# Two sums for the first layer's experts, and the next layer's preparation ahead of the last down projection

## The chip, the cores and the metric

The kernel runs on one core of one Trainium2 chip. The metric is the device time of one execution in microseconds; the time before is the median of three runs.

## What is computed

The reference is a backbone of two layers over 512 latent tokens and 256 context tokens of 1024 numbers. Layer 0 mixes tokens by pooling, layer 1 by grouped-query attention (16 query heads, 4 key/value heads of 64). Behind each mixer stands a mixture of 16 SwiGLU experts of width 256, two of which take each token. Every sub-layer has its own shift, scale and gate, six vectors per layer from a 1024 x 6144 matrix.

```python
for i in range(DEPTH):
    sh1, sc1, g1, sh2, sc2, g2 = adaln(c, w_mod[i], b_mod[i])
    a_lat = modulate(x, norm1_g[i], sh1, sc1)
...
    x = x + g1 * y_lat
    x = x + g2 * hier_moe(modulate(x, norm2_g[i], sh2, sc2), ...)
```

```python
a = jnp.einsum('nd,edf->nef', hf, w_gate)
b = jnp.einsum('nd,edf->nef', hf, w_up)
hid = jax.nn.silu(a) * b * gates.astype(h.dtype)[..., None]
return jnp.einsum('nef,efd->nd', hid, w_down).reshape(shp)
```

Layer 0 runs over all 768 rows (context first, two tiles of 128 rows, then four latent tiles). In layer 1 the context only gives keys and values.

## The kernel before

All is float32. A large product splits each operand into a rounded high part (ScalarE's cast, L464) and a low rest (VectorE's subtraction, L465) and takes three matmuls (`mm3`, L468 to L470).

**Weights.** Each weight load is 1 MB and goes through SP's queue in one fixed order (`order`). `fill` issues the next one as soon as a slot is free; `cap` says how many slots may be used. Behind the first layer's experts the order is: key weights (`qkv` 4), value weights (`qkv` 5), the modulation chunks 2 and 3 of layer 1 (two halves each), the four query weights.

**Modulation.** `mod_row` makes one chunk of 512 modulation numbers: 16 matmuls L404 on two halves of weights, a bias matmul L409, a cast on ScalarE (L411), a subtraction on VectorE (L413). `mod_spread` brings a chunk to all partitions: a matmul L426 for latent and context each, then a copy (L429) for the shift, or for the scale a product with the norm's gain (L395, L423, L431).

**Experts.** `place` finds each expert's rows, `fetch` gathers them from hD by an indirect DMA on POOL's queue (L726), `turn` transposes and splits them, `ups_steps` splits the weights, `up` does gate and up projection (L468 to L470), `turn_hidden` transposes the hidden rows. `down` takes the gate product on VectorE (L767) into one of two y buffers, eight matmuls L772, two products L773, and adds y to accD in DRAM by an indirect DMA that accumulates (L774, the scatter). In turn e the loop runs up(e), turn(e+1), down(e-1), turn_hidden(e); the last down, of expert 15, stands behind the loop. accD holds the residual rows, written by the pooling stage (L961); every scatter of the layer goes to it, so each waits until the one before has landed.

**Hooks.** `experts` calls functions at given turns. Before, chunks 0 and 1 of layer 1's modulation come at turns 13 and 14; `last`, behind the last down, splits key and value weights (`split_w`) and makes chunks 2 and 3. Then follows a loop for overflowing experts, whose number of turns is read at run time; at its end all engines meet. It runs no turn with these inputs.

**Start of layer 1.** Behind that loop `load_rows` brings row tiles of accD, `mod_spread` spreads the four chunks, and for each tile `norm` (a square sum on ScalarE, L446, and a root, L1159), `prep` (VectorE), `turn_rows` (transposes, casts, subtractions) and the projections to keys and values follow. The key projection of tile 0 is the first `mm3` of the layer.

Of the kernel before, what the change touches and what calls it, by code (L numbers as in the profile page):

```python
# [20 lines left out]
D = 1024  # L21
S = 512
L = 256
NT = 6
# [17 lines left out]
BESIDE = (4, 6)  # L42
CAPS = dict(pool=6, moe0=(7,) * 11 + (5,), qkv=4, query=2, attend=(2, 2, 3, 4), wo=3, moe1=(7, 7, 6, 5))

# [181 lines left out]
def backbone(ctx: ExitStack, tc: tile.TileContext, a: dict, out: bass.AP):  # L226
# [244 lines left out]

    hD = dram.tile([NT * 128, D], F32, name="hD")
    accD = dram.tile([NT * 128, D], F32, name="accD")


    class Moe:
# [187 lines left out]
        def up_units(self, e):  # L664
            while len(self.ring) < 6:
                self.more_units()
            return [self.ring[(4 * e + q) % 6] for q in range(4)]

# [92 lines left out]
        def down(self, e, hT, wd):  # L761
# [6 lines left out]
            for half in range(2):  # L768
                cols = slice(512 * half, 512 * half + 512)
                p = pb.get("y", [n, 512])  # L770
                for k in range(2):
                    T.matmul(p, hT[:, k, :], wd[:, k, cols], start=k == 0, stop=k == 1)  # L772
                V.tensor_mul(y[:, cols], p, gs[:, cols])  # L773
            G.indirect_dma_start(out=self.acc, out_offset=bass.IndirectOffsetOnAxis(ap=self.slots[e][0], axis=0),  # L774
                                 in_=y, in_offset=None, bounds_check=self.nt * 128 - 1, oob_is_err=False,
# [162 lines left out]
    def pooled(t):  # L938
# [20 lines left out]
        if t == NT - 1:  # L959
            done("pool")  # L960
        nc.sync.dma_start(accD[t * 128:t * 128 + 128, :], x[t])  # L961

    def norm2(t):
# [98 lines left out]

    sm = ar.scope()
    mod1 = partB + [sm.tile([128, 512], F32R) for _ in range(2)]
    wkv = {}

    def mod1_row(*chunks):
        for c in chunks:
            for _ in mod_row(1, c, mod1[c]):
                pass  # L1070

    def last():
        state["until"] = ("qkv", 0)
        cap(CAPS["qkv"])
        for c in (4, 5):
            wkv[c] = [split_w(c, q) for q in range(4)]
        ar.swap("mid")
        for _ in range(2):
            m0.more_units()
        mod1_row(2, 3)  # L1080

    m0.experts(accD, CAPS["moe0"], more, {
        11: tables, 12: lambda: state.update(mid=0), 13: lambda: mod1_row(0), 14: lambda: mod1_row(1), NE: last})
    m0.sb.free()
# [5 lines left out]
    vv = ab.tile([128, NT, 256])  # L1090
    sx = ar.scope()
    xb = [sx.tile([128, D]) for t in range(4)]
    x = [xb[t % 4] for t in range(NT)]

    def load_rows(t):
        nc.sync.dma_start(x[t], accD[t * 128:t * 128 + 128, :])

    for t in range(4):
        load_rows(t)
    fill()  # L1100
    bc = {(n, v): sx.tile([128, D]) for n in ("B", "A") for v in range(2)}
    pb.split(m=(4, 1), t=(4, 1))
    for c in range(4):
        for _ in mod_spread(sm, 1, c // 2, c % 2, mod1[c], {v: bc["BA"[c // 2], v] for v in range(2)}):
            pass
    sm.free()
# [79 lines left out]
    def store_key(t):  # L1186
        for kv in range(0, 4, 2):
# [3 lines left out]
            A.copy(kT[:, kv:kv + 2, :, t * 128:t * 128 + 128], p2.rearrange("p (a b) c -> p a b c", a=2))  # L1191

    norm(0)
    norm(1)
    prep(0)
    norm(2)
    prep(1)
    turn_rows(0)
    load_rows(4)
    for t in range(NT):  # L1200
        PK[t] = pb.get("k", [128, 256])
        project(PK[t], t, wK)
        if t:
            key(t - 1)
            A.copy(vv[:, t - 1, :], PV[t - 1])
        if t + 1 < NT:
            turn_rows(t + 1)
            if t + 5 < NT:
                load_rows(t + 5)
        square_heads(sk, PK[t], ks[:, t, :])  # L1210
        A.activation(ks[:, t, :], ks[:, t, :], AF.Sqrt, scale=1.0 / HEAD, bias=eps)
        norm(t + 3)
        prep(t + 2)
        PV[t] = pb.get("v", [128, 256])
        project(PV[t], t, wV)
        if t:
            store_key(t - 1)
# [232 lines left out]
    m1.route()  # L1450
    m1.experts(o_rows, CAPS["moe1"], more)
    m1.sb.free()
# [40 lines left out]
```

## Time and profile before

| what | value |
|---|---|
| runs | 931.27 us median (929.12 to 934.59) |
| profiled execution | 933.5 us, span 931.7 us |
| TensorE (PE) | 799.8 us, 86% of the span |
| VectorE (DVE) | 614.5 us, 66% |
| ScalarE (ACT) | 479.1 us, 51% |
| GpSimd (POOL) | 175.4 us, 19% |
| DMA | 204.80 MB, mean 220 GB/s |

The share of busy time is an average over stages with different limits, so a change is read from the stage in which it lies: the experts of layer 0 run from about 150 to 331 us, the preparation of layer 1 from there to about 380. In a timeline a row gives start, duration, engine, line and operation, and in brackets how long the engine was idle before and what ended that. A time is counted from the start of the span. L12 is line 12 of the kernel before.

### The profile page before, as it was taken

To read this page: it belongs to the slowest core of one execution; us is meant where nothing else is said; L and a number is where in the kernel's file an instruction comes from. 1 tells how busy PE (TensorE), PEld (TensorE's weight loads), DVE (VectorE), ACT (ScalarE), POOL (GpSimd) and SP (SyncE) were. 2 spreads that over 40 slices of the span, in tenths; PEclk is the share of its full clock that TensorE was granted. 3 is DMA by queue.
4 is the path that set the end of the run, shared out by engine and by line. 5 is a ranking of instruction groups with operands and counts; after the bars stand their busy time and mean duration, and the time that the engine had idled before them with its cause. 6 is when DMAs were issued, how large, how long until landed. Compare 5 with 4: busy or idle time off the path is not lost. (4 is left out here: it accounts for less than half of the span.)

```text
span 931.7 us, 12772 instructions
## 1 busy us (share of the span) xinstructions
PE 799.8 (86%) x4593; PEld 543.3 (58%) x4593; DVE 614.5 (66%) x1077; ACT 479.1 (51%) x1003; POOL 175.4 (19%) x164
## 2 busy tenths in 40 slices
PE   4699947989998864998787999999999489999993
PEld 0256725566776431997776666556677255566561
DVE  3552875799988734665666677768536768888761
ACT  2534344445555323565558777768623454455440
POOL 1051332122233410002310000001200312322211
PEclk9899976999999995899999999999999789999997
DMA  8997388799999887301100434220136789899962
GB/s 330 417 361 299 136 299 325 262 321 358 370 359 304 311 239 264 126 1 57 80 2 0 181 100 172 91 91 1 46 148 269 282 291 325 305 338 338 345 218 31
DMA packets 36722, 204.80 MB, mean 220 GB/s; under 512 B 6660, under 2 KB 6740, under 8 KB 16816
## 3 DMA queue, kind: packets, MB, share of 16 engines
q1 hardware_dynamic: 24976, 172.06, 48.4%
q0 software_dynamic: 10032, 27.30, 11.6%
q10 hardware_dynamic: 1648, 4.60, 1.3%
q8 instruction: 37, 0.61, 0.3%
q14 instruction: 29, 0.24, 0.1%
HBM read 187.15 MB, written 25.17 MB: 228 GB/s over the span
## 5 line engine op out<-in xcount | busy, mean ns | idle before, releaser
L468 PE MATMUL banks<-low 128*128 128x512 f32 (+2 forms) x404 | 155.1, 384 | 5.7 <-DVE main L1142 4.4
L469 PE MATMUL banks<-low 128*128 128x512 f32 (+2 forms) x404 | 150.2, 372 | 1.1 <-DVE low L465 1.1
L470 PE MATMUL banks<-low 128*128 128x512 f32 (+2 forms) x404 | 150.1, 372 | 0.0
L465 DVE TENSOR_TENSOR low<-main,low 128x1024 fp32r<-128x1024 f32 (+1 forms) x119 | 127.7, 1131 | 14.9 <-ACT low L464 14.7
L464 ACT CAST low<-main 128x1024 fp32r<-128x1024 f32 (+1 forms) x135 | 117.0, 930 | 2.3 <-issue 1.3
L1329 DVE TENSOR_REDUCE main<-banks 128x1 f32<-128x768 f32 x64 | 61.2, 956 | 43.5 <-PE banks L1325 43.3
L468 PEld LDWEIGHTS banks<-low 128*128 128x128 f32 (+1 forms) x404 | 74.6, 185 | 24.1 <-ACT low L464 6.5
L772 PE MATMUL banks<-main 128*128 128x512 f32 (+1 forms) x176 | 82.6, 614 | 3.3 <-ACT low L464 3.3
L469 PEld LDWEIGHTS banks<-low 128*128 128x128 f32 (+1 forms) x404 | 74.7, 185 | 16.2 <-DVE low L465 1.7
L470 PEld LDWEIGHTS banks<-low 128*128 128x128 f32 (+1 forms) x404 | 74.2, 184 | 16.9 <-DVE low L465 0.4
L1347 ACT COPY main<-banks 128x384 f32<-128x384 f32 x128 | 55.9, 486 | 33.6 <-PE banks L1346 33.2
L465 POOL TENSOR_TENSOR low<-main,low 128x512 fp32r<-128x512 f32 x16 | 20.7, 1296 | 273.5 <-ACT low L464 273.5
L404 PE MATMUL banks<-main,cT 128*32 128x512 f32 x376 | 56.8, 707 | 15.0 <-DVE low L413 7.1
L1350 ACT ACTIVATE main<-banks,main 128x768 f32<-128x768 f32 x64 | 63.7, 995 | 8.1 <-DVE main L1333 3.3
L758 ACT COPY main<-banks 128x256 f32<-128x256 f32 (+1 forms) x32 | 11.1, 346 | 100.7 <-PE banks L756 93.2
L773 DVE TENSOR_TENSOR main<-banks,main 128x512 f32<-128x512 f32 (+1 forms) x64 | 42.7, 686 | 27.6 <-PE banks L772 26.0
L459 PE MATMUL banks<-ident,main 128*128 128x128 f32 (+2 forms) x384 | 50.0, 274 | 12.7 <-DVE main L1167 5.5
L1346 PE MATMUL banks<-ident,main 128*128 128x128 f32 x384 | 54.3, 275 | 4.2 <-ACT mid L1234 2.1
L726 POOL DMA_INDIRECT main<-hD,main x32 | 39.8, 1245 | 89.6 <-issue 33.8
L1358 PE MATMUL banks<-main 128*64 128x256 f32 x384 | 53.8, 394 | 2.0 <-DVE low L1336 2.0
L772 PEld LDWEIGHTS banks<-main 128*128 128x128 f32 (+1 forms) x176 | 31.0, 185 | 39.1 <-issue 34.2
L459 PEld LDWEIGHTS banks<-ident,main 128*128 128x128 f32 (+2 forms) x384 | 42.3, 146 | 18.7 <-DVE main L1167 6.3
(255 smaller groups left out, 1479.4 us busy)
## 6 DMA issues: line engine op xcount, KB each, us to landing
main<-in_moe_wgu_dram SPq DMA_DIRECT2D x49, 1024.0 KB
main<-in_w_mod_dram SPq DMA_DIRECT2D x47, 1024.0 KB
main<-in_moe_wd_dram SPq DMA_DIRECT2D x22, 1024.0 KB
mid<-in_moe_wgu_dram SPq DMA_DIRECT2D x15, 1024.0 KB
mid<-in_moe_wd_dram SPq DMA_DIRECT2D x10, 1024.0 KB
main<-in_attn_wqkv_dram SPq DMA_DIRECT2D x6, 1024.0 KB
hD<-main POOLq DMA_DIRECT2D x9, 512.0 KB, 4.5
main<-in_attn_wo_dram SPq DMA_DIRECT2D x4, 1024.0 KB
```

The source lines that it names most:

```text
L404: T.matmul(p[32 * j:32 * j + 32, :], cT[:, 4 * h + j, :], w[:, j, :], start=h == 0, stop=h == 1)
L459: T.transpose(p[:, k, :], src[:, c * 128:c * 128 + 128], ident[:n, :n])
L464: A.copy(hi, src)
L465: eng.tensor_sub(lo, src, hi.bitcast(F32))
L468: T.matmul(p, xh, wh, start=first, stop=False)
L469: T.matmul(p, xh, wl, start=False, stop=False)
L470: T.matmul(p, xl, wh, start=False, stop=last)
L772: T.matmul(p, hT[:, k, :], wd[:, k, cols], start=k == 0, stop=k == 1)
L1329: V.reduce_max(m[:, 0:1], p, axis=AX.X)
L1346: T.transpose(p2[:, j, :], Ps[u][:, k * 128:k * 128 + 128], ident)
L1347: A.copy(PT[u // 4, hh][:, 3 * g3:3 * g3 + 3, 128 * q2:128 * q2 + 128], p2)
L1350: A.activation(Ps[step], p, AF.Exp, bias=mx[step][:, 0:1], scale=rq, accum_out=mx[step][:, 1:2])
```

## The change

There is a second array accB in DRAM. The pooling stage sets it to zero, a tile at a time, by copies from a zero input on ScalarE's queue; the scatter of an even expert goes to accD, that of an odd one to accB. Layer 1 reads both and adds them: tiles 0 and 1 on VectorE, the others on POOL, which then are stored back to accD for the later residual. The accB rows come through two buffers in turn, so the row of tile t+2 is loaded when tile t is merged.

Turn 14 makes chunk 1 and splits the key weights; turn 15, which still lies ahead of the last down, makes chunk 2, splits the value weights and spreads chunks 0 and 1; `last` makes chunk 3, spreads 2 and 3 and runs a square root on a constant. The rotation of the weight units is shifted by two, so that the units that the key and value splits overwrite are free by then. The slots for the start of layer 1 go from 4 to 3.

```diff
-CAPS = dict(pool=6, moe0=(7,) * 11 + (5,), qkv=4, query=2, attend=(2, 2, 3, 4), wo=3, moe1=(7, 7, 6, 5))
+CAPS = dict(pool=6, moe0=(7,) * 11 + (5,), qkv=3, query=2, attend=(2, 2, 3, 4), wo=3, moe1=(7, 7, 6, 5))
...
+    accB = dram.tile([NT * 128, D], F32, name="accB")
...
-            return [self.ring[(4 * e + q) % 6] for q in range(4)]
+            return [self.ring[(4 * e + q + 2) % 6] for q in range(4)]
...
-            G.indirect_dma_start(out=self.acc, out_offset=bass.IndirectOffsetOnAxis(ap=self.slots[e][0], axis=0),
+            G.indirect_dma_start(out=self.acc[e % len(self.acc)], out_offset=bass.IndirectOffsetOnAxis(ap=self.slots[e][0], axis=0),
...
         nc.sync.dma_start(accD[t * 128:t * 128 + 128, :], x[t])
+        nc.scalar.dma_start(accB[t * 128:t * 128 + 128, :], a["zero"])
...
+    def spread1(*chunks):
+        for c in chunks:
+            for _ in mod_spread(sm, 1, c // 2, c % 2, mod1[c], {v: bc["BA"[c // 2], v] for v in range(2)}):
+                pass
+
+    def keys():
+
+        state["until"] = ("qkv", 0)
+        mod1_row(1)
+        wkv[4] = [split_w(4, q) for q in range(4)]
+
+    def values():
+
+        pb.split(t=(2, 1), y=(2, 1), m=(4, 1))
+        mod1_row(2)
+        wkv[5] = [split_w(5, q) for q in range(4)]
+        bc.update({(n, v): sx.tile([128, D]) for n in ("B", "A") for v in range(2)})
+        spread1(0, 1)
+
     def last():
-        state["until"] = ("qkv", 0)
         cap(CAPS["qkv"])
-        for c in (4, 5):
-            wkv[c] = [split_w(c, q) for q in range(4)]
+        mod1_row(3)
+        spread1(2, 3)
+        pb.split(t=(2, 1), u=(2, 1), y=(2, 1), i=(1, 1), m=(1, 1))
+
+        A.activation(sm.tile([128, 1]), eps, AF.Sqrt)
         ar.swap("mid")
         for _ in range(2):
             m0.more_units()
-        mod1_row(2, 3)
-
-    m0.experts(accD, CAPS["moe0"], more, {
-        11: tables, 12: lambda: state.update(mid=0), 13: lambda: mod1_row(0), 14: lambda: mod1_row(1), NE: last})
+
+    m0.experts((accD, accB), CAPS["moe0"], more, {
+        11: tables, 12: lambda: state.update(mid=0), 13: lambda: mod1_row(0), 14: keys, 15: values, NE: last})
...
+    zb = [sx.tile([128, D]) for t in range(2)]
...
+    def load_more(t):
+        nc.sync.dma_start(zb[t % 2], accB[t * 128:t * 128 + 128, :])
+
+    def merge(t, eng=V):
+
+        if t < NT:
+            eng.tensor_add(x[t], x[t], zb[t % 2])
+            if t > 1:
+                nc.scalar.dma_start(accD[t * 128:t * 128 + 128, :], x[t])
+            if t + 2 < NT:
+                load_more(t + 2)
+
+    for t in range(2):
+        load_rows(t)
+        load_more(t)
+    for t in range(2, 4):
         load_rows(t)
     fill()
-    bc = {(n, v): sx.tile([128, D]) for n in ("B", "A") for v in range(2)}
-    pb.split(m=(4, 1), t=(4, 1))
-    for c in range(4):
-        for _ in mod_spread(sm, 1, c // 2, c % 2, mod1[c], {v: bc["BA"[c // 2], v] for v in range(2)}):
-            pass
...
+    merge(0)
     norm(0)
+    merge(1)
     norm(1)
     prep(0)
+    merge(2, G)
     norm(2)
     prep(1)
     turn_rows(0)
...
+        merge(t + 3, G)
         norm(t + 3)
...
-    m1.experts(o_rows, CAPS["moe1"], more)
+    m1.experts((o_rows,), CAPS["moe1"], more)
```

The order of the instructions changes at three places. The first is VectorE from the last up projection to the overflow loop. Before (L749 is the hidden product of expert 15, the first L767 and L773 are of the down of expert 14, L465 x8 splits key and value weights, L413 ends chunks 2 and 3, L834 reads the loop's count):

```order
L749 SCALAR_TENSOR_TENSOR main<-main,banks 128x256
L767 SCALAR_TENSOR_TENSOR main<-main 128x1024
L773 TENSOR_TENSOR main<-banks,main 128x512 x2
L767 SCALAR_TENSOR_TENSOR main<-main 128x1024
L773 TENSOR_TENSOR main<-banks,main 128x512 x2
L465 TENSOR_TENSOR low<-main,low 128x512 x8
L413 SCALAR_TENSOR_TENSOR low<-partA,neg,banks 128x512 x2
L834 TENSOR_LOAD main
```

Now (L751, L769 and L775 are the old L749, L767 and L773):

```order
L465 TENSOR_TENSOR low<-main,low 128x512 x4
L751 SCALAR_TENSOR_TENSOR main<-main,banks 128x256
L769 SCALAR_TENSOR_TENSOR main<-main 128x1024
L775 TENSOR_TENSOR main<-banks,main 128x512 x2
L413 SCALAR_TENSOR_TENSOR low<-partA,neg,banks 128x512
L465 TENSOR_TENSOR low<-main,low 128x512 x4
L769 SCALAR_TENSOR_TENSOR main<-main 128x1024
L775 TENSOR_TENSOR main<-banks,main 128x512 x2
L413 SCALAR_TENSOR_TENSOR low<-partA,neg,banks 128x512
L431 SCALAR_TENSOR_TENSOR main<-banks,main 128x512 x4
L836 TENSOR_LOAD main
```

The key splits moved ahead of expert 15's hidden product, chunk 2 and the value splits ahead of its down, and the scale's spread (L431) ahead of the loop.

The second place is SP's queue behind the overflow loop, now (L1121 loads accD rows, L1124 accB rows, L290 weights; before there were four accD rows, four query weights, two accD rows):

```order
L1121 DMA main<-accD 128x1024
L1124 DMA main<-accB 128x1024
L1121 DMA main<-accD 128x1024
L1124 DMA main<-accB 128x1024
L1121 DMA main<-accD 128x1024 x2
L290 DMA main<-in_attn_wqkv_dram 128x2048 x3
L1124 DMA main<-accB 128x1024 x3
L1121 DMA main<-accD 128x1024 x2
L1124 DMA main<-accB 128x1024
L290 DMA main<-in_attn_wqkv_dram 128x2048
```

The accB rows of tiles 2 to 4 stand behind three query weights, and the accD rows of tiles 4 and 5 behind those.

The third place is ScalarE behind the loop. Before (L446 and L1159 are a tile's norm, L464 the casts of the transposed rows):

```order
L446 ACTIVATE main<-main 128x1024
L1159 ACT_TABLE_LOAD
L1159 ACTIVATE main<-main,eps 128x1
L446 ACTIVATE main<-main 128x1024
L1159 ACTIVATE main<-main,eps 128x1
L446 ACTIVATE main<-main 128x1024
L1159 ACTIVATE main<-main,eps 128x1
L464 CAST mid<-banks 128x512 x4
```

Now (L1194 is the old L1159, L1131 the store of a merged tile, here tile 2):

```order
L446 ACT_TABLE_LOAD
L446 ACTIVATE main<-main 128x1024
L1194 ACT_TABLE_LOAD
L1194 ACTIVATE main<-main,eps 128x1
L446 ACTIVATE main<-main 128x1024
L1194 ACTIVATE main<-main,eps 128x1
L1131 DMA accD<-main 128x1024
L446 ACTIVATE main<-main 128x1024
L1194 ACTIVATE main<-main,eps 128x1
L464 CAST mid<-banks 128x512 x4
```

A store that needs the merged tile 2 came in ahead of the norm of tile 2 and of the first casts, and there is one table load more.

## Rows read from the trace of the kernel before

**Rows 1.** busy us of PE, PEld, DVE, ACT, POOL, then PEclk, DMA share, GB/s
```profile
205.00:280.00 75.00, 75.00 (x359) 52.84 (x358) 69.90 (x93) 41.91 (x60) 24.05 (x14) 1.00 1.01 363
280.00:331.00 51.00, 45.99 (x207) 29.27 (x205) 37.29 (x46) 19.68 (x30) 17.52 (x13) 1.00 0.90 307
```

**Rows 2.** who waited for whom, 205 to 331: total us, times, longest
```profile
POOL accD L774 <- DMA accD<-main: 63.7, 8, 11.3
...
PE banks L459 <- DMA main<-hD,main: 3.5, 2, 1.9
```

**Rows 3.** the gate products of line L767: ns min/median/max, first and last start
```profile
L767 DVE SCALAR_TENSOR_TENSOR main<-main x16: 1272/1284/1286, 175.9 to 344.6; 128x1024 f32<-128x1024 f32 x16
```

**Rows 4.** landing of line L774's scatters, issued 200 to 300, then 345 to 376
```profile
DMA to landing us min/median/max: 10.0/10.6/12.2
...
DMA to landing us min/median/max: 6.2/6.5/6.7
```

**Rows 5.** timeline of POOL, 315 to 360: start us, us, instruction [idle before]
```profile
323.76 1.99 POOL L774 DMA_INDIRECT accD<-main  x1 [11.33 <-DMA accD<-main]
...
352.72 1.55 POOL L774 DMA_INDIRECT accD<-main  x1 [5.42 <-DVE low L465]
```

**Rows 6.** timeline of PE, from the last down but one to the attention
```profile
330.85 3.60 PE L772 MATMUL banks<-main 128*128 128x512 f32 x8
...
338.01 5.37 PE L772 MATMUL banks<-main 128*128 128x512 f32 x8 [3.34 <-ACT low L464]
...
355.08 1.94 PE L404 MATMUL banks<-main,cT 128*32 128x512 f32 x8 [0.35 <-DMA main<-in_w_mod_dram]
```

**Rows 7.** timeline of SP, 324 to 360
```profile
324.98 25.05 SPq L290 DMA_DIRECT2D main<-in_w_mod_dram  x4
...
359.85 0.34 SPq L1096 DMA_DIRECT2D main<-accD  x1
```

**Rows 8.** timeline of DVE, 331 to 360
```profile
344.59 1.29 DVE L767 SCALAR_TENSOR_TENSOR main<-main 128x1024 f32<-128x1024 f32 x1 [6.09 <-DMA accD<-main]
...
345.98 1.29 DVE L773 TENSOR_TENSOR main<-banks,main 128x512 f32<-128x512 f32 x2
...
347.19 4.90 DVE L465 TENSOR_TENSOR low<-main,low 128x512 fp32r<-128x512 f32 x8
...
358.39 0.75 DVE L413 SCALAR_TENSOR_TENSOR low<-partA,neg,banks 128x512 fp32r<-128x512 f32 x1 [5.65 <-ACT partA L411]
```

**Rows 9.** timeline of ACT, 367 to 374
```profile
368.64 1.28 ACT L1159 ACT_TABLE_LOAD   x1
...
371.50 1.04 ACT L446 ACTIVATE main<-main 128x1024 bf16<-128x1024 f32 x1
...
372.95 0.58 ACT L464 CAST mid<-banks 128x512 fp32r<-128x512 f32 x1
```

**Rows 10.** stretches behind the first row load
```profile
360.00:368.00 8.00, 5.82 (x10) 2.74 (x10) 3.16 (x5) 3.70 (x7) 0.00 (x0) 0.50 0.84 304
368.00:378.00 10.00, 5.66 (x24) 5.15 (x25) 5.79 (x8) 6.03 (x12) 0.00 (x0) 0.50 1.01 424
```

**Rows 11.** POOL and DVE beside each other; the key and value stage
```profile
104.63 2.35 POOL L506 TENSOR_TENSOR main<-low 128x1024 f32<-128x1024 f32 x1 [1.72 <-DVE r L1002]
...
104.80 3.27 DVE L511 SCALAR_TENSOR_TENSOR main<-main,r,low 128x1024 f32<-128x1024 f32 x1 [0.18 <-PE banks L459]
...
380.00:400.00 20.00, 20.00 (x173) 20.00 (x172) 15.54 (x28) 15.29 (x50) 0.00 (x0) 1.00 0.01 4
```

**Rows 12.** a w_mod load of the first layer and its use
```profile
67.31 0.33 SPq L290 DMA_DIRECT2D main<-in_w_mod_dram  x1
...
80.36 1.92 PE L404 MATMUL banks<-main,cT 128*32 128x512 f32 x16
```

**Rows 13.** a w_mod load behind others and its use
```profile
24.31 7.37 SPq L290 DMA_DIRECT2D main<-in_w_mod_dram  x4
...
39.02 1.94 PE L404 MATMUL banks<-main,cT 128*32 128x512 f32 x8 [3.18 <-DMA main<-in_w_mod_dram]
```

More of the change, by code (lines that the diff above doesn't have):

```diff
@@ L1060, in split_w @@
         return u
-    sm = ar.scope()
+    sm, sx = ar.scope(), ar.scope()
     mod1 = partB + [sm.tile([128, 512], F32R) for _ in range(2)]
@@ L1070, in mod1_row @@
                 pass
+    bc = {}
+    def spread1(*chunks):
[12 more added lines that the diff above has]
+        spread1(0, 1)
     def last():
-        state["until"] = ("qkv", 0)
         cap(CAPS["qkv"])
-        for c in (4, 5):
-            wkv[c] = [split_w(c, q) for q in range(4)]
+        mod1_row(3)
+        spread1(2, 3)
+        pb.split(t=(2, 1), u=(2, 1), y=(2, 1), i=(1, 1), m=(1, 1))
+        A.activation(sm.tile([128, 1]), eps, AF.Sqrt)
         ar.swap("mid")
@@ L1090, in backbone @@
     vv = ab.tile([128, NT, 256])
-    sx = ar.scope()
     xb = [sx.tile([128, D]) for t in range(4)]
     x = [xb[t % 4] for t in range(NT)]
+    zb = [sx.tile([128, D]) for t in range(2)]
     def load_rows(t):
         nc.sync.dma_start(x[t], accD[t * 128:t * 128 + 128, :])
-    for t in range(4):
+    def load_more(t):
[11 more added lines that the diff above has]
+    for t in range(2, 4):
         load_rows(t)
     fill()
-    bc = {(n, v): sx.tile([128, D]) for n in ("B", "A") for v in range(2)}
-    pb.split(m=(4, 1), t=(4, 1))
-    for c in range(4):
-        for _ in mod_spread(sm, 1, c // 2, c % 2, mod1[c], {v: bc["BA"[c // 2], v] for v in range(2)}):
-            pass
     sm.free()
@@ L1482 @@
     given["band"] = band_table()
+    given["zero"] = np.zeros((128, D), np.float32)
     given["rope"] = rope_table()
```

## Prediction

> **What bounds the kernel now.** I read the stages first (busy time by stretch), then who waited for whom in the first layer's experts, then the engines' timelines from the last expert to the first key projection, since every edit ends there.
>
> In the steady part of the expert loop TensorE is busy 75.00 of 75.00 us, beside DMA engines at a share of 1.01; from 280 to 331 it is busy 45.99 of 51.00, at 0.90 [rows 1]. So 5.0 us of TensorE time is lost in the second stretch. POOL waited 63.7 us, 8 times, for an earlier scatter into accD before it could issue the next, and TensorE 3.5 us for gathers of token rows, which POOL issues behind those scatters [rows 2]. A scatter lands 10.0 to 12.2 us after its issue while weights stream, 6.2 to 6.7 at the end [rows 4], and the next may start only then. That period is longer than an expert's matmuls, so the scatters fall behind: number 12 (counted from 0) is issued at 323.76 after 11.33 us of waiting, number 15 at 352.72 [rows 5], 22 us after the last up projection ended at 330.85 [rows 6].
>
> Behind it comes a tail of 29.0 us, from 330.85 to the first row load of the next layer at 359.85 [rows 6, 7]. The reader is to see two chains that end together. One is the scatters: 352.72 plus 6.2 to 6.7 is 358.9 to 359.4. The other is the modulation: VectorE takes the gate product of expert 15 only at 344.59, after 6.09 us for a scatter to free the y buffer, then eight key/value splits in 4.90 us; these free a weight slot, so the last w_mod load goes out at the end of a 25.05 us stretch of issues, TensorE asks for it at 355.08, and VectorE ends the row at 359.14 [rows 6 to 8]. From the first row load to ScalarE's first cast for the attention takes another 13.10 us (359.85 to 372.95) [rows 7, 9].
>
> **Part 1, two sums: -5.0 us.** Scatter e now waits for scatter e-2 only. Sixteen gate products, one an expert, begin between 175.9 and 344.6 [rows 3], 11.2 us apart on average with all waits; two experts are far longer than the 12.2 us of a landing, so POOL and the gathers no longer wait. The gain is between 0 (DMA engines full) and the 5.0 us of idle; I take 5.0, because with a share of 1.01 the first stretch kept TensorE at 75.00 of 75.00. The last up then ends at 325.85.
>
> **Part 2, the tail: -5.9 us.** Key splits go behind modulation row 1, row 2 and the value splits ahead of the last down, row 3 behind it. ScalarE's and VectorE's key splits (half of 4.90 us) stand ahead of the last up's activation in their queues and are hidden by that up, if the key weights are there; else it waits for them. What is late next is the second half of row 2's weights. The first w_mod load goes out at 324.98 [rows 7], so at 320; ahead and with it are some 1.5 MB of key/value weights (an estimate), both halves (2.1 MB) and a scatter (0.5 MB): 4.1 MB at 307 GB/s is 13.4 us, at 363 GB/s 11.3 [rows 1]. I take 333.4. From second half to finished row took 4.06 us (355.08 to 359.14) where eight matmuls took 1.94; with the faster ones, 16 in 1.92 [rows 12], it is about 2.8: 336.2 to 337.5. Then VectorE: four value splits 2.45, gate product 1.29, two products 1.29 [rows 8]: 341.2 to 342.5. TensorE in that time runs four spread matmuls and the eight of the last down, and eight took 3.60 and 5.37 [rows 6], ending by some 342.5, so at most 343. The last scatter lands 6.2 to 6.7 later, and the rows are loaded 0.5 to 0.9 after that, as before: 347.9 to 350.6. Row 3 with its spreads runs beside this landing. I take 349, against 359.85: 10.85 us earlier, 5.0 of it from part 1.
>
> **Part 3, reading two sums: +10.2 us.** The rows are now accD plus accB, through two buffers. SP's queue gets six row loads (3.15 MB), three query weights (3.15 MB), and only then the accB row of tile 2, since its buffer is free only after the merge of tile 0. On ScalarE the store of merged tile 2 and its norm stand ahead of the first casts, which tile 0's key projection needs. So this projection waits for the merge of tile 2. At the old rates [rows 10] 2.43 MB have landed 8.15 us after the first row load, and the other 4.39 MB take 10.4 us at 424 GB/s: 18.5. At 304 GB/s throughout it would be 22.4. I take 19.2, near the lower end, as the old stretch held 424 for ten us. POOL's merge takes 2.35, as its 128x1024 product does [rows 11], the norm 1.45 (371.50 to 372.95) [rows 9], the store's issue and hand-overs about 0.3 (estimate): 23.3 us, where it was 13.10. The other bound is -2: behind a merged tile 0 at about 5.5, ScalarE's three norms (1.45 each) and a table load (1.28) end at about 11 if tile 2 does not keep them (the second rival goes that way). After the first cast the stage is TensorE's, 20.00 of 20.00 [rows 11].
>
> **At nothing.** The six zero copies into accB: two fall where w_mod streams, 1.05 MB or 2.5 us at 424 GB/s; the w_mod load issued at 67.31 is used from 80.36 [rows 12], a lead of 13 us that hides them (2.5 us if it did not). The table load for the square root ahead of the overflow loop: the loop's body holds loads of its own, so behind it the program loads twice, at L446 and at the norm (1.28 us each [rows 9]). It saves nothing; both stand inside the wait for tile 2, and would cost 1.28 us without it. The other rotation of weight units moves addresses. The store of merged rows runs where DMA engines are at 0.01 [rows 11]. The fourth query weight is loaded later, but used only by the fourth group of query projections, hidden by three groups.
>
> POOL's other three merges run beside VectorE. VectorE's 128x1024 product took 3.27 us beside POOL's, where its kind takes 1.29 [rows 8, 11]: it waited POOL's operation out. VectorE has 4.46 us free in 20.00 [rows 11], so I charge nothing; all three in full would be 7.0 us, 2.6 beyond the free time. The Trainium skill (SBUF — State Buffer, Who interferes with whom) has it as a rule: a VectorE instruction with two SBUF inputs and a GpSimd one that reads SBUF exclude each other for the whole instruction. By it, with every merge met, the sum would be +1.9 us, and without it -0.7; the trace agrees on the one pair seen.
>
> **Sum.** -5.0 - 5.85 + 10.2 = -0.65 us. The profiled execution took 933.5 us, so 932.9; the median shown is 2.2 lower, 931.27, so **930.6 us**: no change.
>
> **Rivals.**
> - *DMA engines become the bound (slower).* 0.90 of 51.00 us is 45.9 us of full use; 2.1 MB of w_mod that was loaded behind 331 now falls ahead of it, 5.8 us at 363 GB/s. That is 51.7 us of work in 46, so part 1 gives 0, and the last scatter lands like a loaded one, 10.6 instead of 6.5 us. It decides when row 3's second half lands after the last down, about 342. Price +5.0 + 4.1: 939.7. For it: the share of 1.01. Against: the loads of the tail have slots earlier than their use. Chance 0.22.
> - *The merge's row does not wait behind the query weights (faster).* Issued 6 us after the first row load, it lands at about 10, the cast comes at 14.1, and part 3 costs 1.0: 921.4. Against it: the first of four w_mod loads issued from 24.31 on, behind others, was waited for until 39.02, 14.7 us [rows 13]. Chance 0.12. The Trainium skill (DMA: Bandwidth & Descriptors, Queues, rings and completion order) says each DMA engine consumes a queue's descriptors in ring order; this row agrees.
> - *No load is late in the tail (faster).* TensorE could take row 2's second half at 325.85 + 3.60 for a down + 1.4 for a transpose and the first half, 330.8, so the tail ends 2.6 us earlier: 928.0. Against it: the share of 0.90 ahead of it, with these loads added. Chance 0.15; a third of it counts as faster.
> - *POOL's merges hold VectorE up*: +2.6, 933.2. Chance 0.10.
>
> **How the numbers follow.** The forecast has 0.41. A measurement of this kernel tells about 0.5%, 4.7 us, from no change. Faster: 0.12, a third of the third rival, 0.06 of the forecast's edge: 0.23. Slower: the first rival and 0.04 of the forecast's edge: 0.26. Same: 0.51. The range 923 to 939 leaves out most of the second rival and half of the first.
>
> **What would show it.** Right: POOL's waits for scatters nearly gone, TensorE without idle from 205 to the last up, row loads at about 349, and then ScalarE waiting until 23 us after the first row load, with the first cast near the old 372.95. Wrong: row loads later than 354 (part 2), a first cast within 16 us of the first row load (part 3), or TensorE waiting for w_mod before 90 us.

## The result, and the profile after

The changed kernel takes **947.13 us** (median of 4 runs, 944.23 to 948.76), the kernel before beside it 930.92 (4 runs, 929.12 to 934.59): ratio 1.016, 95% interval 1.0125 to 1.0196. It is slower by 1.6%, outside the range of 923 to 939. The profiled execution has a span of 945.4 us, where before had 931.7.

To see where 13.7 us went I cut both spans at the same seven places: the hidden product of expert 1 and of expert 14 in the first layer (VectorE, L749, after L751), the first row load (SP, L1096, after L1121), ScalarE's first cast for the attention (L464), the last four attention products (TensorE, L1358, after L1397), the products that place the rows of layer 1's expert 1 (TensorE, L695, after L697), and the hidden product of expert 1 in layer 1. Experts are counted from 0.

| stage, us | before | after | difference |
|---|---|---|---|
| start to expert 1 | 168.61 | 164.77 | -3.84 |
| expert 1 to expert 14 | 148.84 | 144.34 | -4.50 |
| expert 14 to first row load | 42.40 | 45.72 | +3.32 |
| first row load to first cast | 13.10 | 23.49 | +10.39 |
| first cast to last attention products | 314.58 | 315.21 | +0.63 |
| last attention products to placing | 50.12 | 56.11 | +5.99 |
| placing to expert 1 of layer 1 | 30.27 | 32.36 | +2.09 |
| rest | 163.78 | 163.40 | -0.38 |

The first line is no gain of the change: this stage took 162.45 to 169.35 us over all executions below, in no order that fits an edit.

**Expert loop.** Stretches of the kernel after, columns as in [rows 1], and who waited for whom from 201 to 323 (us in total, times, longest):

```profile
201.00:276.00 75.00, 75.00 (x359) 52.84 (x359) 73.33 (x96) 41.93 (x60) 24.82 (x15) 1.00 1.01 362
276.00:323.00 47.00, 44.88 (x204) 29.01 (x202) 33.63 (x43) 19.70 (x30) 13.61 (x13) 1.00 0.95 325
```
```profile
POOL accB L776 <- DVE main L775: 32.9, 5, 11.3
...
POOL accD L776 <- DVE main L775: 12.4, 5, 2.5
```

POOL no longer waits for a scatter [rows 2], only for the product that it is to scatter, and TensorE loses 2.1 of 47 us where it lost 5.0 of 51 [rows 1].

**Tail.** SP, its longest wait from 312 to 345, ScalarE, TensorE and POOL of the kernel after, and three stretches (columns as in [rows 1]):

```profile
315.31 1.57 SPq L290 DMA_DIRECT2D main<-in_attn_wqkv_dram  x2
317.41 19.34 SPq L290 DMA_DIRECT2D main<-in_w_mod_dram  x4
354.83 0.34 SPq L1121 DMA_DIRECT2D main<-accD  x1
...
358.10 1.65 SPq L290 DMA_DIRECT2D main<-in_attn_wqkv_dram  x3
361.12 15.73 SPq L1124 DMA_DIRECT2D main<-accB  x3
```
```profile
SPq L290 <- DMA main<-in_attn_wqkv_dram: 11.1, 1, 11.1
```
```profile
328.84 2.18 ACT L464 CAST low<-main 128x512 fp32r<-128x512 f32 x4 [10.39 <-DMA main<-in_attn_wqkv_dram]
330.93 0.37 ACT L749 ACTIVATE main<-banks 128x256 f32<-128x256 f32 x1
...
376.93 1.06 ACT L446 ACTIVATE main<-main 128x1024 bf16<-128x1024 f32 x1 [11.32 <-POOL main L1129]
...
378.32 1.05 ACT L464 CAST mid<-banks 128x512 fp32r<-128x512 f32 x2
```
```profile
332.44 0.69 PE L758 MATMUL banks<-ident,main 128*128 128x128 f32 x2 [5.55 <-DVE main L751]
334.43 1.94 PE L404 MATMUL banks<-main,cT 128*32 128x512 f32 x8 [1.30 <-DVE main L775]
336.84 1.94 PE L404 MATMUL banks<-main,cT 128*32 128x512 f32 x8 [0.48 <-DMA main<-in_w_mod_dram]
...
341.55 5.09 PE L774 MATMUL banks<-main 128*128 128x512 f32 x8
```
```profile
347.65 1.55 POOL L776 DMA_INDIRECT accB<-main  x1 [10.85 <-DVE main L775]
374.17 4.63 POOL L1129 TENSOR_TENSOR main<-main 128x1024 f32<-128x1024 f32 x2 [24.97 <-DMA main<-accB]
```
```profile
323.00:328.00 5.00, 3.89 (x10) 1.54 (x9) 0.00 (x0) 0.00 (x0) 0.00 (x0) 1.00 0.85 265
328.00:333.00 5.00, 0.56 (x2) 0.29 (x2) 3.51 (x6) 2.46 (x5) 0.00 (x0) 0.79 0.42 170
333.00:338.00 5.00, 3.22 (x17) 0.40 (x16) 1.87 (x3) 0.37 (x1) 1.55 (x1) 0.50 0.99 380
```

Read from above: the key weights go out at 315.31 and ScalarE can split them only at 328.84, 13.5 us later. Behind those casts, in its queue, stands the activation of expert 15 (330.93), behind that the transposes (TensorE idle 5.55). SP too waits for the key weights, 11.1 us, since the second half of row 2 is to go into their slot once they are split: it goes out at 332.02 (one of the four of the second line), and TensorE takes it at 336.84. While it waits, the DMA engines fall to a share of 0.42 (328 to 333); TensorE comes back from its idle time at the lower of its two clock levels (0.50 from 333 on). The last down projection starts at 341.55, the last scatter goes out at 347.65, and the rows are loaded at 354.83: 5.0 us earlier than before [rows 7], where 8.3 had been won up to expert 14. Then ScalarE stands still for 11.32 us until POOL has merged tile 2, whose second row waited behind three query weights.

**Late loss.** SP, ScalarE's queue, VectorE and TensorE of the kernel after behind the attention, and two stretches:

```profile
694.27 3.60 SPq L290 DMA_DIRECT2D main<-in_moe_wgu_dram  x2
```
```profile
694.24 1.85 ACTq L1430 DMA_DIRECT2D main<-accD  x4
```
```profile
706.03 0.69 DVE L1442 TENSOR_TENSOR main<-main 128x512 f32<-128x512 f32 x1 [1.30 <-DMA main<-accD]
...
709.81 0.69 DVE L1442 TENSOR_TENSOR main<-main 128x512 f32<-128x512 f32 x1 [2.29 <-DMA main<-accD]
```
```profile
706.49 0.39 PE L468 MATMUL banks<-low 128*128 128x512 f32 x1
711.16 0.79 PE L469 MATMUL banks<-low 128*128 128x512 f32 x1 [4.28 <-DVE low L465]
711.75 0.63 PE L470 MATMUL banks<-low 128*128 128x512 f32 x1
```
```profile
695.00:710.00 15.00, 11.88 (x53) 9.49 (x51) 9.79 (x16) 4.79 (x9) 0.00 (x0) 0.99 1.00 397
710.00:720.00 10.00, 8.84 (x31) 6.85 (x32) 6.76 (x12) 3.73 (x6) 0.00 (x0) 0.67 0.98 400
```

The same stretches of the kernel before, its SP, and its rows in ScalarE's queue:

```profile
690.00:705.00 15.00, 13.78 (x62) 10.83 (x62) 13.78 (x22) 5.38 (x10) 0.00 (x0) 1.00 0.98 396
705.00:715.00 10.00, 10.00 (x64) 7.93 (x63) 5.26 (x9) 5.50 (x10) 0.62 (x1) 1.00 0.67 269
```
```profile
615.23 42.94 SPq L290 DMA_DIRECT2D main<-in_moe_wgu_dram  x2
691.54 2.69 SPq L290 DMA_DIRECT2D main<-in_w_mod_dram  x2
```
```profile
688.29 1.79 ACTq L1391 DMA_DIRECT2D main<-accD  x4
```

Before, the first two expert weights of layer 1 went out at 615 and 658, during the attention. Now they go out at 694, together with the four rows of the residual. VectorE waits 3.6 us for two of these rows, the splits behind it are late, TensorE idles 4.28 us and comes back at the lower of its two levels (granted clock 0.67 over 710 to 720; a 128x512 product 0.63 us instead of 0.39). In all, the stretch from the last attention products to the placing is 6.0 us longer.

Most of the 2.1 us behind the placing is another thing. Sixteen products of a modulation row take 3.62 us here (granted clock 0.67 over 769.5 to 774.5) and 1.92 us before (1.00), behind the same 1.74 us of idle time. The kernel e1 below, whose rows are not late, has this too. The two lines are of after and of e1:

```profile
771.16 3.62 PE L404 MATMUL banks<-main,cT 128*32 128x512 f32 x16 [1.74 <-ACT main L429]
```
```profile
755.18 3.43 PE L404 MATMUL banks<-main,cT 128*32 128x512 f32 x16 [1.74 <-ACT main L429]
```

### The profile page after: what moved, and what is told of

It is laid out like the page before. It is cut to its first block, busy times and chain, and to the rows that moved or that the text cites. A ratio compares the mean times of both kernels' runs of the same rounds, so it can differ in the third digit from the quotient of the medians.

```text
span 945.4 us, 12823 instructions
## 1 busy us (share of the span) xinstructions
PE 800.7 (85%) x4593; PEld 543.5 (57%) x4593; DVE 618.4 (65%) x1079; ACT 482.1 (51%) x1006; POOL 181.4 (19%) x168
## 3 DMA queue, kind: packets, MB, share of 16 engines
q0 software_dynamic: 10032, 27.30, 11.1%
## 5 line engine op out<-in xcount | busy, mean ns | idle before, releaser
L465 DVE TENSOR_TENSOR low<-main,low 128x1024 fp32r<-128x1024 f32 (+1 forms) x123 | 131.8, 1128 | 25.4 <-ACT low L464 25.2
L464 ACT CAST low<-main 128x1024 fp32r<-128x1024 f32 (+1 forms) x139 | 121.2, 934 | 13.8 <-DMA main<-in_attn_wqkv_dram 10.4
L774 PE MATMUL banks<-main 128*128 128x512 f32 (+1 forms) x168 | 78.8, 614 | 0.4 <-ACT main L760 0.4
L465 POOL TENSOR_TENSOR low<-main,low 128x512 fp32r<-128x512 f32 x16 | 20.8, 1298 | 245.4 <-ACT low L464 245.4
L775 DVE TENSOR_TENSOR main<-banks,main 128x512 f32<-128x512 f32 (+1 forms) x64 | 42.9, 687 | 29.0 <-PE banks L774 27.4
L760 ACT COPY main<-banks 128x256 f32<-128x256 f32 (+1 forms) x32 | 11.1, 347 | 96.5 <-PE banks L758 89.0
L728 POOL DMA_INDIRECT main<-hD,main x32 | 37.9, 1184 | 105.6 <-issue 50.8
L1397 PE MATMUL banks<-main 128*64 128x256 f32 x384 | 53.8, 394 | 2.0 <-DVE low L1375 2.0
L468 PE MATMUL banks<-low,mid 128*128 128x256 f32 x128 | 38.0, 297 | 14.0 <-ACT mid L464 10.3
```

Of the source, the lines that this page charges most:

```text
L464: A.copy(hi, src)
L465: eng.tensor_sub(lo, src, hi.bitcast(F32))
L468: T.matmul(p, xh, wh, start=first, stop=False)
```

## Experiments

Each was timed beside the kernel before on the same chip. Stages in us, from one profiled execution each (A: expert 1 to 14, B: expert 14 to first row load, C: to the first cast, D: to the last attention products, E: to the placing, F: to expert 1 of layer 1):

| kernel | A | B | C | D | E | F | median | ratio to before (95%) |
|---|---|---|---|---|---|---|---|---|
| before | 148.84 | 42.40 | 13.10 | 314.58 | 50.12 | 30.27 | 930.92 | |
| after | 144.34 | 45.72 | 23.49 | 315.21 | 56.11 | 32.36 | 947.13 | 1.0160 (1.0125 to 1.0196) |
| e1 | 148.73 | 42.21 | 12.82 | 314.28 | 50.30 | 32.08 | 932.59 | 1.0005 (0.9976 to 1.0034) |
| e2 | 144.38 | 41.03 | 23.46 | 312.76 | 50.13 | 31.76 | 935.31 | 1.0049 (1.0027 to 1.0071) |
| e3 | 144.36 | 46.53 | 23.38 | 314.18 | 55.86 | 32.60 | 947.97 | 1.0206 (1.0164 to 1.0248) |
| e4 | 144.53 | 46.42 | 16.66 | 314.18 | 56.58 | 32.22 | 938.79 | 1.0088 (1.0054 to 1.0121) |
| e5 | 144.36 | 43.25 | 23.72 | 313.53 | 56.09 | 32.59 | 944.86 | 1.0119 (1.0063 to 1.0175) |
| e6 | 148.63 | 44.72 | 8.86 | 313.33 | 56.11 | 31.87 | 936.81 | 1.0044 (1.0011 to 1.0077) |
| e7 | 144.34 | 37.94 | 23.30 | 312.96 | 50.11 | 30.25 | 932.05 | 1.0014 (0.9984 to 1.0044) |
| e8 | 144.36 | 43.09 | 23.99 | 313.62 | 49.88 | 30.50 | 938.53 | 1.0062 (1.0033 to 1.0091) |
| e9 | 144.37 | 43.27 | 17.75 | 314.06 | 49.73 | 30.18 | 930.19 | 0.9982 (0.9951 to 1.0014) |
| e10 | 144.35 | 38.35 | 17.60 | 318.84 | 50.10 | 30.01 | 931.41 | 0.9975 (0.9944 to 1.0007) |
| e11 | 144.30 | 37.61 | 18.12 | 313.75 | 50.28 | 30.55 | 928.19 | 0.9981 (0.9958 to 1.0004) |
| e12 | 144.35 | 43.51 | 15.14 | 312.63 | 49.71 | 30.28 | 929.97 | 0.9981 (0.9956 to 1.0007) |

My first theory named three losses: the moved splits wait for their weights, tile 2's merge waits behind query weights, and one query weight slot less makes all later loads late.

**e1, before with three slots.**
```diff
-CAPS = dict(... qkv=4, ...)
+CAPS = dict(... qkv=3, ...)
```


> The kernel before with one edit: three instead of four weight slots while the next layer's query weights are fetched. Theory (the late loss of the change comes from here): in the changed kernel the fourth query weight was loaded at 428.52 and everything behind it in SP's list came one step later (first w_mod of that stage at 444.34 instead of 423.82, first expert weight of layer 1 at 694.27 instead of 615.23); the first cast stood 5.4 us behind the old one, the end 13.7, so 8 us were lost between. This edit alone then gives +6 to +9 us, 937 to 940, with the first expert weight of layer 1 loaded near 690. Rival (the late loss comes from the merges, their stores and the clock, not from the slots): 929 to 933.

The rival holds: no difference in the time, first expert weight at 611.15, E 50.30. The slot count is not the late loss in E. F is 32.08 all the same: it is 30.0 to 30.6 in before and e7 to e12 and 31.8 to 32.6 in after and e1 to e6, by the clock level of the sixteen products above (1.92 or 1.93 us, 3.43 to 3.62). No run shows what decides that.

**e2, before with the two sums only.** The scatters by turns, zero copies, merges, `qkv=3`; `keys`, `values` and the spreads stay where they were.

> The kernel before with the two sums alone (scatters by turns, zero copies, reading of both, three weight slots because the two row buffers take the room of the fourth), while modulation and key/value splits stay where they were. Theory: the expert loop gains 4 to 8 us, the last scatter goes out about 6 us earlier than 352.72 because gate product 15 waits for no scatter, the first cast comes 23 us after the first row load, and the late loss is there too: 8 - 6 - 5 + 10 + 8 does not add up twice for the same wait, so in all +5 to +12 us, 936 to 943. Rival (the moved splits are what costs, the two sums gain): under 928.

Slower by 0.49%, 4.6 us, a little under the theory's range. C is as it said; what it said of the late loss is wrong, with E at 50.13: that comes neither with the slots nor with the two sums. POOL and SP:
```profile
334.54 1.75 POOL L775 DMA_INDIRECT accB<-main  x1 [2.83 <-DVE main L774]
```
```profile
352.79 0.34 SPq L1099 DMA_DIRECT2D main<-accD  x1
```
The last scatter goes out 18 us before the old 352.72 [rows 5], yet the rows come only at 352.79: the overflow loop stands behind modulation row 3 on every engine, and the row loads behind the loop.

**e3, after with late key splits.**
```diff
 def keys():
...
-    wkv[4] = [split_w(4, q) for q in range(4)]
 def values():
...
+    wkv[4] = [split_w(4, q) for q in range(4)]
     mod1_row(2)
```


> The changed kernel with the four key splits moved back behind expert 15's activation, ahead of modulation row 2. Theory: the 10.4 us that ScalarE waited for the key weights ahead of that activation go away; expert 15's hidden product stands at 323 to 325 instead of 331.91, the first row load at 349 to 352 instead of 354.83, and the time is 3 to 6 us shorter than the changed kernel's 947.1: 941 to 944. Rival (DMA engines bound the tail, so the wait only moves to row 2's or row 3's weights): the first row load stays within 1 us of 354.83, and the time within 2 us of 947.

The rival holds, if the row load is counted from expert 1: it comes at 360.24 in an execution that reached expert 1 4.6 us later than the changed kernel's, so 0.8 us later than 354.83 on the same footing. ScalarE's wait is gone (expert 15 follows expert 14 in 14.67 us instead of 22.80), and TensorE waits for the modulation's weights instead, ahead of the last down projection. The DMA engines are nearly full in that wait (share 0.94 from 333 to 338, 1.01 from 338 to 343):
```profile
338.38 1.94 PE L404 MATMUL banks<-main,cT 128*32 128x512 f32 x8 [6.81 <-DMA main<-in_w_mod_dram]
343.19 1.94 PE L404 MATMUL banks<-main,cT 128*32 128x512 f32 x8 [2.88 <-DMA main<-in_w_mod_dram]
```

**e4, after with the second sum's rows first.**
```diff
     for t in range(2, 4):
         load_rows(t)
-    fill()
...
     merge(1)
+    fill()
```


> The changed kernel with the second sum's rows of tiles 2 and 3 ahead of the three query weights in SP's list, instead of behind them. Theory: the merge of tile 2 waited behind 3.15 MB of query weights (23.5 us from the first row load to the first cast, 12 of them for that); with the rows first the cast comes 13 to 16 us after the first row load, and the time is 7 to 10 us shorter than 947.1: 937 to 940. The query weights are asked for some 50 us later and stay hidden. Rival (the time goes into the merges, norms and issues themselves, or is taken back later when query weights and stores come late): the first cast stays 20 us or more behind the first row load, or the end gains under 3 us.

The theory's direction, a little short of its size (13 to 16 us for C, 7 to 10 us in all): C falls by 6.8 us to 16.66, the ratio by 0.72%, 6.7 us (give or take some 4.5 us, by the two intervals). No later stage takes it back. SP:
```profile
362.46 3.10 SPq L1124 DMA_DIRECT2D main<-accB  x2
365.61 1.39 SPq L290 DMA_DIRECT2D main<-in_attn_wqkv_dram  x3
```

**e5, after with the extra slot moved.** After e1 and e2 the late loss belonged to the moved order. There, as I read the layout, the vectors are placed ahead of the value rows, and a small tile comes to lie on one of the extra weight slots.
```diff
-EXTRA = (33952, 29376)
+EXTRA = (33952, 28352)
```


> The changed kernel with one number edited: the second extra weight slot of the attention stage lies at word 28352 instead of 29376. In the changed kernel the two sets of vectors are placed ahead of the value rows, so a small tile comes to lie at 30656 and blocks the slot at 29376 for the whole stage: the first expert weight of layer 1 was loaded at 694.27, together with the rows for the residual, and TensorE took 56.1 us from the last attention product to the router's last product where the kernel before (first expert weight at 615.23), the three-slot kernel and the two-sums kernel all took 50.1 to 50.3. Theory: with the slot free again this stretch is 50 to 52 us, and the time 4 to 6 us shorter than 947.1: 941 to 943. Rival (the stretch is longer for another reason, such as the clock or the stores of merged rows): it stays at 55 or more, and the time within 2 us of 947.

One expert weight goes out earlier, the other does not, and E does not move:
```profile
664.16 30.76 SPq L290 DMA_DIRECT2D main<-in_moe_wgu_dram  x2
```
```profile
DVE main L1442 <- DMA main<-accD: 3.3, 2, 2.3
```
The second of the two (its issue ends at 664.16 + 30.76 = 694.92) still meets the rows, and VectorE still waits 3.3 us for them. What holds its slot until then is open. The median is 2.3 us lower, with intervals that overlap.

**e6, the moved order with one sum.** The change without `accB` and merges, `qkv=4`, `EXTRA = (33952, 31904)`.

> The changed kernel with the moved modulation and splits alone: one sum in DRAM as before, no merge, four weight slots for the query weights, and the extra slot placed where it is free (word 31904). Theory: the moved order costs by itself, since TensorE asks for row 2's weights ahead of the last down projection, and ScalarE for the key weights ahead of expert 15's activation, while both still stream: from expert 14's hidden product to the first row load 45 to 49 us, where the kernel before took 42.4; from the first row load to the first cast 11 to 13; in all +2 to +6 us, 933 to 937. Rival (my recorded step: moving it saves, because scatters and modulation run beside each other): the first row load comes 3 to 6 us earlier than 359.85, 925 to 928.

The total is as the theory said (0.44%, 4.1 us), the places are not: B is 2.3 us longer than before, C 4.2 shorter (the vectors are ready), so the moved order saves 1.9 us up to the first cast when the two sums don't stand in its way. Then E costs 6.0: here too one expert weight goes out with the residual rows (685.34 beside 685.36), and VectorE waits 4.1 us.

**e8, after with the residual rows first.**
```diff
-    cap(CAPS["wo"])
...
-            nc.scalar.dma_start(x[t], accL[t * 128:t * 128 + 128, :])
+            nc.sync.dma_start(x[t], accL[t * 128:t * 128 + 128, :])
+        cap(CAPS["wo"])
```


> The changed kernel with one edit: the four residual row loads of the output projection go out on SP's queue ahead of the next expert weights, instead of on ScalarE's queue at the same time as these. Moving the slot alone left the stretch from the last attention product to the router's last product at 56.1 us: one of the two expert weights then still went out at 694.9, beside the rows at 694.6, and VectorE still waited 3.3 us for a row. Theory (the rows arrive late because one or two megabytes of weights go out beside them): with the rows first VectorE does not wait for them, the stretch takes 50 to 52.5 us, and the time is 941 to 944. Rival (the stretch is longer for a reason that lies in the moved order itself, and the wait for a row is only where it shows): the stretch stays at 55 or more, and the time within 2 us of 947.

E is 49.88, as before the change (6.2 us less than after), F 30.50, and the ratio falls by 0.98%, 9.1 us (give or take some 4 us). SP and the stretches:
```profile
662.26 15.73 SPq L1429 DMA_DIRECT2D main<-accD  x4
692.32 2.26 SPq L290 DMA_DIRECT2D main<-in_moe_wgu_dram  x2
```
```profile
693.00:708.00 15.00, 14.20 (x64) 11.20 (x63) 13.73 (x22) 5.13 (x10) 0.00 (x0) 1.00 0.96 365
708.00:718.00 10.00, 10.00 (x62) 7.92 (x61) 5.89 (x10) 5.50 (x10) 0.63 (x1) 1.00 0.74 303
```
The granted clock stays at 1.00. In SP's list the rows also go out up to 32 us earlier, so the run by itself does not tell whether the weights beside them made them late or their own issue. Other runs do. Before, the rows go out 0.8 us behind the last attention products, in the changed kernel 0.7, and before VectorE does not wait for them. In e2 and e7 both expert weights go out 16 us or more ahead of the rows, and E is 50.1; in e5 and e6 one of two goes out with the rows, and E is 56.1. So, by these comparisons, the weights beside the rows make them late.

**e9, after with both rows first** (e4 and e8 together).

> The changed kernel with two edits together: the second sum's rows of tiles 2 and 3 ahead of the query weights, and the residual rows ahead of the expert weights. Theory (two separate losses): 8.3 us from the one, as measured, and 4 to 6 from the other, so 933 to 936; what is left above the kernel before is the moved order, with 44 to 47 us from expert 14's hidden product to the first row load and 16.7 from there to the first cast. Rival (they share a cause, or the second is not there): 938 to 940.

A little better than the theory: 930.19, level with before, 1.78% or 16.6 us below the changed kernel, where e4 and e8 alone gave 6.7 and 9.1. The two losses are separate and add up. What is left cancels: A gains 4.5 us on before, B and C lose 5.5.

**e7, e10, e11: two sums with the modulation behind the loop.** e2, with the second sum's rows first; e7 puts `mod1_row(2, 3)` behind the row loads and the merges of tiles 0 and 1, e10 only `mod1_row(3)` ahead of the merges, and e11 is e10 with
```diff
-    merge(2, G)
+    merge(2)
...
-        merge(t + 3, G)
+        merge(t + 3)
```


> The two-sums kernel (splits and rows 2 and 3 not moved ahead of the last down projection) with two edits: modulation rows 2 and 3 come behind the overflow loop and behind the row loads instead of ahead of them, and the rows of the second sum for tiles 2 and 3 are loaded ahead of the query weights. In the two-sums kernel the last scatter went out at 334.54, but the first row load came only at 352.79, when row 3 was done. Theory: the first row load comes at 342 to 344, the merges of tiles 0 to 2 are done by 353, the modulation still ends at 352 and its spreads at 359, and the first cast comes at 362 to 366 instead of 376.25 (372.95 in the kernel before): 10 to 13 us less than the two-sums kernel's 935.3, so 922 to 925, faster than before by 0.7 to 1.0%. Rival (the modulation's weights are late because the DMA engines are full, and row loads ahead of them only make them later): the first cast comes at 370 or later, 929 to 932.

> The two-sums kernel with modulation row 2 left ahead of the overflow loop, row 3 behind it, ahead of the merges, and the second sum's rows ahead of the query weights. With both rows behind the loop (the run before) TensorE waited 16.07 us at the loop, the first row load came at 346.66, and the modulation was then in the way: first cast at 369.96. Theory: row 2 fits into that wait, the first row load stays at 346 to 348, row 3 is done by 351, the spreads by 358, and the first cast comes at 362 to 365; 5 to 8 us less than 932.05, so 924 to 927. Rival (the rest of the chain, norm and spreads, sets the cast anyway): first cast at 368 or later, 930 to 932.

> The run before (two sums, row 3 behind the loop, second rows first) with all merges on VectorE instead of tiles 2 to 5 on POOL. In the run before VectorE's operations stretched beside POOL's merges (2.47 and 3.37 us where 1.29 and 1.22 are usual), and from the first cast to the last attention product it took 318.8 us where the other kernels took 312.8 to 315.2. Theory (POOL's merges hold VectorE up in the middle of its busiest stretch): 312.5 to 315 us again, the first cast no later, the time 4 to 7 us less than 931.4: 924 to 927. Rival (the four added merges of 1.23 us on VectorE cost what the stretching did): 929 to 932.

e7: the rows come at 346.66, but the first cast only at 369.96, as the rival had it: TensorE stands until the last scatter has landed and the last modulation weight is there (SP waits 4.7 us for the one, then 2.1 for the other), and takes the modulation rows afterwards.
```profile
347.00 3.64 PE L404 MATMUL banks<-main,cT 128*32 128x512 f32 x16 [16.07 <-DMA main<-in_w_mod_dram]
```
e10: the time is the rival's (931.41), its reason is not. This execution reached expert 1 4.9 us later than e7's; counted from there the first cast, 369.58, stands at 364.7, inside the theory's 362 to 365, and B and C together are 5.3 us shorter than in e7. But D grew by 5.9 us over e7's 312.96. VectorE and POOL in e10, then the same two lines of VectorE in e11:
```profile
365.84 2.47 DVE L1185 SCALAR_TENSOR_TENSOR main<-main 128x1024 f32<-128x1024 f32 x1
368.23 3.37 DVE L1183 TENSOR_TENSOR main<-main 128x1024 f32<-128x1024 f32 x1
```
```profile
363.84 3.38 POOL L1106 TENSOR_TENSOR main<-main 128x1024 f32<-128x1024 f32 x1 [24.13 <-DMA main<-accB]
367.45 3.07 POOL L1106 TENSOR_TENSOR main<-main 128x1024 f32<-128x1024 f32 x1 [0.23 <-DMA main<-accB]
```
```profile
362.98 1.28 DVE L1185 SCALAR_TENSOR_TENSOR main<-main 128x1024 f32<-128x1024 f32 x1
...
365.31 1.22 DVE L1183 TENSOR_TENSOR main<-main 128x1024 f32<-128x1024 f32 x1
```
Without POOL's merges VectorE is at its usual lengths and D back at 313.75, 5.1 us less in these executions. In the ratios (0.9975, 0.9981) no gain is left (e10's profiled execution, 934.16, was one of its longest), so what the merges cost over many executions stays open.

**e12, e9 with the merges on VectorE.**

> The changed kernel with the second sum's rows ahead of the query weights and the residual rows ahead of the expert weights, as in the run that took 930.2, and all merges on VectorE. Theory of the POOL merges as the kernels show it: here VectorE was slowed only once (3.42 us where 1.23 is usual), so moving the merges gains 0 to 2 us: 928 to 930. Rival (they hold VectorE up here as much as in the other order): 923 to 926.

929.97, the ratio as in e9, so the ratios show no cost of POOL's merges. In the one profile of each, C and D together are 4.0 us shorter than in e9; as with e11, this stays open.

No kernel is shown to beat the kernel before: e9 to e12 stand at 0.9975 to 0.9982, each with 1 inside its interval. The stages A to F of e11 and e12, with all merges on VectorE, add up to 594.6 and 595.6 us where before has 599.3, but that is one execution each.

## Why the prediction was wrong

**Part 1 was right** (-5.0; measured -4.5 up to expert 14). Stage A is 148.6 to 148.8 in the three kernels with one sum and 144.3 to 144.5 in all with two.

**Part 2 failed** (-5.85; here +3.3). Over all executions B is 43.1 to 46.5 with the moved order and both sums, and 41.0 to 42.4 with the old one, so the size varies, the sign does not. The size goes with the clock behind the wait: where B is 43.1 to 43.5 the eight products of the last down projection took 3.6 us, where it is 45.7 to 46.5 they took 4.1 to 5.1. Here they took 5.09; in e9:

```profile
338.12 3.59 PE L774 MATMUL banks<-main 128*128 128x512 f32 x8
```

Two steps broke. "hidden by that up, if the key weights are there; else it waits for them": I named the condition and charged nothing, though the key weights go out only 8 us before that up ends, and they took 13.5. And "I take 333.4" for row 2's second half was made from megabytes over a rate, as if all loads were issued together. The second half needs the slot that the key splits free, so a late key weight held it back until 332.02, while the DMA engines had room (share 0.42). Counted from the end of the last up, it came after 13.5 us and not after 7.6. A smaller miss is the row's finish: 4.06 us again, where I had taken 2.8 for faster products. e3 shows that it is not the splits' place alone: with them out of the way TensorE waits 6.81 and 2.88 us for row 2, and the last down projection stands behind that. Row 2 was put ahead of work that had all it needed. The sign that I had named for this, row loads later than 354, came: 354.83 (358.7, had this execution reached expert 1 as late as before's).

**Part 3 was right** in mechanism and size (+10.2; measured +10.39; 23.3 forecast from row load to first cast, 23.49 measured). e4 shows the reason: with the rows ahead of the query weights 6.8 us of it go. The Trainium skill (DMA: Bandwidth & Descriptors, Queues, rings and completion order) says that each DMA engine takes a queue's descriptors in ring order; e4, where only the order in SP's list differs, agrees.

**What was missing** is a term as large as part 2's forecast: E, +6.0 us. The prediction ended at the first cast; "After the first cast the stage is TensorE's" was borne out by D (+0.6) and said nothing of what comes behind the attention. I charged the fourth query weight at nothing, rightly (e1), but had not asked what else lies elsewhere in SBUF once the vectors are placed earlier, nor which loads stand next to each other when a slot comes free later. That the weights beside the rows cost the time is shown by e8 with e2, e5, e6 and e7. That the layout makes the expert weights late is read from the layout; e5 shows it for one of the two only. F's +2.1 is a clock level that e1 and e2 have without late rows; it stays open. The zero copies cost nothing that shows: TensorE waits 4.1 us for w_mod up to 90 us, before 4.4.

**The rivals.** The slower one (DMA engines as the bound, 939.7) was nearer to the result. Its two prices did not come: part 1 did not fall to 0, and the last scatter landed 6.3 us after its issue, not 10.6. But full engines are part of part 2's miss: the share was 0.85 from 323 to 328, while the key weights were still on their way, and 0.94 and 1.01 in e3's wait. The two faster ones did not come either: row 2's second half was late, and the accB row of tile 2 went out at 361.12 and was there at 374.17. POOL's merges, the fourth rival, met VectorE in this kernel once (an L1200 took 3.42 us instead of 1.22), and D grew by 0.6. In e10, where they fall into VectorE's chain, its operations took 2.47 and 3.37 us instead of 1.28 and 1.22. The Trainium skill (SBUF — State Buffer, Who interferes with whom) has the two engines exclude each other for such instructions; the stretched lines of e10 agree.

The ledger, then: -3.8 (the start, which varies), -4.5, +3.3, +10.4, +0.6, +6.0, +2.1, -0.4, together 13.7. I forecast -5.0, -5.85, +10.2.

## What to carry to other kernels

Work that is moved ahead of a projection brings its weights' arrival with it: find for each load which slot it needs and whose last read frees that slot, and take its landing from there, not from bytes over a rate. When a change alters how much is allocated, or in which order, follow the loads of every later stage, not only up to the place where the edits end: here a stage 300 us behind the edits cost 6 us, more than the two sums gained in theirs. Put small loads that someone waits for ahead of large ones that nobody needs yet: two such orders (e4, e8) took back all that this change had lost.

## What I had not expected

Stage "start to expert 1" took between 162.45 and 169.35 us in these executions. In the profile of before the products of the first up projection still take 0.63 us at 149.9, in that of after they are at 0.40 from 146.7 on. That is no work of the change: e1, whose instructions there are those of before, reached expert 1 at 165.42, and e10, with the two sums, at 169.28. The clock level differs in the same way in the tail (the last down projection took 5.1 us in after and 3.6 in e8, whose instructions up to there are the same) and in F (sixteen products, 1.92 us in before and 3.43 in e1). So one stage's granted clock can differ between executions by as much as most edits are worth: stages are to be compared from a mark behind it, and a time counted from the start of the span, as in e3 and e10, misleads.
